# A hybrid attention and GLA step: softmax in merged operations, six split sums, turned keys beside the block scores, two attention steps per product, clock warm-up

## The chip, the cores and the metric

The kernel runs on one core of a Trainium2 chip. The metric is the device time of one execution in microseconds; before the change it is 2342.8 us, the median of 3 runs (2340.0 to 2345.78). A core has five engines that run beside each other, each with its own queue, and wait for one another through semaphores. TensorE (PE) multiplies matrices into PSUM, an accumulator memory of 8 banks; VectorE (DVE), ScalarE (ACT) and GpSimd (POOL) work element by element; SyncE (SP) starts DMA transfers between the chip's main memory and the on-chip memory SBUF.

## The reference, cut to what matters

One step of a two-layer encoder over 2048 prompt frames and 8 x 16 sample frames, width 1024. Each layer has window attention (A) and gated linear attention (GLA, B) side by side:

```python
u = rms_norm(h, norm_g) @ w_in
qa, ka, va, ga, qb, kb, vb, gb, ab = split(u)
qa = partial_rope(rms_norm(qa, q_norm_g), pos)      # 8 heads of 64
ka = partial_rope(rms_norm(ka, k_norm_g), pos)      # 2 heads of 64
# A: softmax over 192 keys, with a sink per head
m = maximum(max(s), sink); pr = exp(s - m)
oa = (pr / (sum(pr) + exp(sink - m))) @ va
# B: per block, b = cumsum(log_sigmoid(ab @ w_gate_up + b_gate) / 16)
att = where(causal, (qb * exp(b)) @ (kb * exp(-b)).T, 0)
ob = att @ vb + (qb * exp(b)) @ S
S = exp(b_last) * S + (kb * exp(b_last - b)).T @ vb
mix = concat([oa * silu(ga), rms_norm(ob, gla_norm_g) * silu(gb)])
h = h + mix @ w_out
h = h + sigmoid(rms_norm(h, pe_norm_g) @ w_pg) * (p @ w_pe)
```

Outputs are y, the last 128 rows of keys and values, and the states S.

## The kernel before, in words

**Tiling.** The 2176 frames are 17 tiles of 128 (the last holds the sample frames). `GROUPS` packs them into five groups of 3, 4, 4, 3 and 3 tiles; the two layers run over the five groups one after the other, 10 groups in all. Each group runs `phase_in` (the projection, attention, GLA, the first half of the output projection) and `phase_out` (the rest of it, the gate, the embedding).

**Products.** Every large product is made of three (`mm3`, L382 to L384), since each float32 operand is split into a rounded high half and a low half: high x high, high x low, low x high. `unit_a` gives 128 output columns for all frames of a group (24 products of 384 or 512 columns), `unit_b` 512 output columns for one tile. Weights come in pieces of 256 KB (`raw`); ScalarE rounds the high half (L212), VectorE subtracts the low half (L95). The weight ring holds five slots, and o-blocks (`o0` to `o3`, 256 columns of `w_out` each) take two.

**Banks.** Of the 8 PSUM banks two are the ring "mm" (`pm`), two the ring "t" (`pt`: transposes and other small products), and four change their use: while attention runs they are two pairs, "s" (scores) and "o" (outputs); elsewhere four single banks "w" (`pw1`).

**What is woven in between.** Attention and GLA are generators; after each large product `pump(n)` advances them by n steps, two lanes in turn, with n set by the table `Z` (`pga` after the attention gate's products). The program's text and these numbers give priorities; a scheduler with a timeline model then fixes each engine's order, so instructions can stand earlier or later than the text has them. On TensorE a queue runs strictly in that order: an instruction that waits holds up all behind it.

**Steps that the change touches.** `softmax` (L547 to L572): maximum, sink, negation (L559), four exponentials on ScalarE, sum, reciprocal, four scalings (L571). `gla_scores` (L823): the chain of block scores into "s", the masked copy `at` (L857), then two transposes of the keys (L860) into a bank of "t", copied to `ke` by ScalarE (L862). `gla_prompt`: output of a block into "o" (from `at` and the state S), the product with `ke` into "t", and S (L924); `gla_norm_gate` makes `on` (L875), `gla_out` transposes it (L886) and makes the second half of the mix (L888, L889). `fin` (L496): transposes of the keys and of the gate's low-rank input `ab`; kT is copied by ScalarE (L500), abT by VectorE (L501); `gate_chain` multiplies abT by `wgu` (L1073). At the end of `phase_in` (L1060 to L1066) the first halves (k 0 to 3, the attention half of the mix) of the first four output sums are made, the last tile's `gla_out` ("tail") before the fourth; `phase_out` adds the second halves and makes the other four sums whole.

## Time and profile before

| what | value |
|---|---|
| median of 3 runs | 2342.8 us |
| the profiled execution | 2341.45 us, its span 2339.7 us |
| TensorE busy | 2261.6 us, 97% |
| VectorE busy | 1622.7 us, 69% |
| ScalarE busy | 1271.1 us, 54% |
| GpSimd busy | 679.8 us, 29% |
| mean granted TensorE clock | 0.995 |
| DMA | 278.94 MB, mean 119 GB/s |

The span goes from the first to the last instruction. In the rows a tile stands as output<-inputs by the names of the program, and L is the line in the kernel before. Behind the bar or in brackets stands the time for which the engine was idle just before the instruction, and what ended that idle time. Matmuls are pipelined, so the durations of neighbours overlap, and the time from start to start is what one costs. A wait for several semaphores is put down to the one that came last.

### The profile page before, as it was taken

The page shows a single profiled execution, that of the slowest core. Times are in us where ns is not written, and L with a number is a line of the kernel's source. Part 1 is how long each engine was busy: PE and PEld are TensorE (multiplying, and loading weights), DVE is VectorE, ACT ScalarE, POOL GpSimd, SP SyncE. Part 2 cuts the span into 40 slices and gives each one's busy share as a digit, 9 for nine tenths or more (in the row PEclk, how much of TensorE's full clock was granted, in tenths as well). Part 3 has the DMA queues.
Part 4 walks back from the last instruction along what each step waited for, and adds up shares of the span by engine and source line. Part 5 has one row for each costly group of instructions (what it writes and reads, how often), then busy time and mean ns, then how long its engine had stood idle before and what let it go on. Part 6 is the DMA issues. An engine that isn't in the chain of part 4 may idle for free.

```text
span 2339.7 us, 41130 instructions
## 1 busy us (share of the span) xinstructions
PE 2261.6 (97%) x14796; PEld 1946.8 (83%) x14796; DVE 1622.7 (69%) x3579; ACT 1271.1 (54%) x2927; POOL 679.8 (29%) x771
## 2 busy tenths in 40 slices
PE   7999999999999999998999999999999999999998
PEld 6889877887778879887988898778877888798878
DVE  7757766768566866775776678667676678577755
ACT  6546544645545655553665556445554556566533
POOL 3124322342224222412331242224312142233222
PEclk9999999999999999999999999999999999999999
DMA  4334313433153425533542543234322443264343
GB/s 153 113 120 148 112 53 111 153 101 109 37 170 120 127 87 165 159 99 104 188 134 84 161 139 96 64 121 142 109 73 73 153 137 108 83 188 142 105 129 100
DMA packets 160236, 278.94 MB, mean 119 GB/s; under 512 B 17648, under 2 KB 43632, under 8 KB 160032
## 3 DMA queue, kind: packets, MB, share of 16 engines
q1 hardware_dynamic: 159344, 275.43, 38.1%
q8 instruction: 116, 1.90, 0.3%
q10 hardware_dynamic: 688, 0.88, 0.1%
q14 instruction: 88, 0.72, 0.1%
HBM read 255.41 MB, written 20.71 MB: 118 GB/s over the span
## 4 chain that ended last, share of the span: by engine, by line
PE 77%; DVE 6%; issue 6%; DMA 4%; ACT 4%; POOL 3%; DVEq 0%; ACTq 0%; POOLq 0%; SPq 0%
PE mm L382 15%; PE mm L384 14%; PE mm L383 14%; PE pw L382 7%; PE pw L383 7%; PE pw L384 7%; PE o L126 3%; DVE w L95 2%; DMA raw<-in_w_pe_dram 2%; PE s L120 2%; PE s L126 2%; POOL xacc L95 1%; DMA raw<-in_w_out_dram 1%; ACT w L212 1%; PE o L120 1%
## 5 line engine op out<-in xcount | busy, mean ns | idle before, releaser
L95 DVE TENSOR_TENSOR w<-raw,w 128x512 fp32r<-128x512 f32 (+1 forms) x800 | 575.3, 744 | 141.1 <-ACT w L212 136.3
L212 ACT ACTIVATE w<-raw 128x512 fp32r<-128x512 f32 (+1 forms) x800 | 471.4, 626 | 240.8 <-PE pw L384 62.5
L95 POOL TENSOR_TENSOR ot<-gth,hst 128x384 f32<-128x384 f32 (+1 forms) x79 | 102.3, 1300 | 290.6 <-DVE gth L1158 266.5
L382 PE MATMUL mm<-B,w 128*128 128x384 f32 (+1 forms) x432 | 156.3, 362 | 1.8 <-DVE gth L1154 1.1
L382 PE MATMUL mm<-A,w 128*128 128x384 f32 (+1 forms) x432 | 155.6, 360 | 1.9 <-DVE gth L1154 1.3
L384 PE MATMUL mm<-B,w 128*128 128x384 f32 (+1 forms) x432 | 156.1, 361 | 0.0
L383 PE MATMUL mm<-B,w 128*128 128x384 f32 (+1 forms) x432 | 155.9, 361 | 0.0
L384 PE MATMUL mm<-A,w 128*128 128x384 f32 (+1 forms) x432 | 155.6, 360 | 0.0
L383 PE MATMUL mm<-A,w 128*128 128x384 f32 (+1 forms) x432 | 155.0, 359 | 0.0
L382 PE MATMUL pw<-mix,w 128*128 128x384 f32 (+1 forms) x384 | 138.4, 366 | 12.0 <-DVE on L875 12.0
L95 POOL TENSOR_TENSOR acc<-sq,acc 128x384 f32<-128x384 f32 (+1 forms) x60 | 74.3, 1239 | 259.7 <-ACT sq L313 259.5
L382 PE MATMUL mm<-w,B 128*128 128x512 f32 (+1 forms) x368 | 141.7, 385 | 0.0
L383 PE MATMUL mm<-w,B 128*128 128x512 f32 (+1 forms) x368 | 141.3, 384 | 0.0
L384 PE MATMUL mm<-w,B 128*128 128x512 f32 (+1 forms) x368 | 140.8, 383 | 0.0
L382 PE MATMUL mm<-w,A 128*128 128x512 f32 (+1 forms) x360 | 139.5, 387 | 0.0
L383 PE MATMUL mm<-w,A 128*128 128x512 f32 (+1 forms) x360 | 138.8, 385 | 0.0
L384 PE MATMUL mm<-w,A 128*128 128x512 f32 (+1 forms) x360 | 138.3, 384 | 0.0
L384 PE MATMUL pw<-mix,w 128*128 128x384 f32 (+1 forms) x384 | 137.4, 358 | 0.0
L383 PE MATMUL pw<-mix,w 128*128 128x384 f32 (+1 forms) x384 | 137.3, 357 | 0.0
L95 POOL TENSOR_TENSOR mix<-ga_t,mix 128x512 fp32r<-128x512 f32 x34 | 53.0, 1560 | 265.6 <-ACT mix L583 265.6
L563 ACT ACTIVATE P<-s,mx 128x192 f32<-128x192 f32 (+3 forms) x272 | 108.7, 412 | 8.6 <-DVE mx L559 8.4
L1155 ACT ACTIVATE gth<-gth 128x384 f32<-128x384 f32 (+2 forms) x81 | 45.0, 560 | 125.7 <-DVE gth L1154 125.5
(320 smaller groups left out, 6378.7 us busy)
## 6 DMA issues: line engine op xcount, KB each, us to landing
raw<-in_w_in_dram SPq DMA_DIRECT2D x400, 256.0 KB, 2.9
raw<-in_w_out_dram SPq DMA_DIRECT2D x160, 256.0 KB, 2.9
raw<-in_w_pg_dram SPq DMA_DIRECT2D x160, 256.0 KB, 3.0
raw<-in_w_in_dram SPq DMA_DIRECT2D x40, 272.0 KB, 3.0
raw<-in_w_pe_dram SPq DMA_DIRECT2D x40, 256.0 KB, 3.3
hl<-in_h_dram SPq DMA_DIRECT2D x24, 192.0 KB, 3.2
hbuf<-ot SPq DMA_DIRECT2D x24, 192.0 KB, 1.9
hx<-hbuf SPq DMA_DIRECT2D x24, 192.0 KB, 3.8
```

The lines of the kernel that those rows point to most:

```text
L95: (eng or G).tensor_tensor(out=out, in0=in0, in1=in1, op=op1)
L120: prev[0] = PE.matmul(**kw).ins
L126: prev[0] = PE.matmul(**kw).ins
L212: A.activation(out=hi, in_=r, func=ACTF.Copy)
L382: PE.matmul(out=out, lhsT=sh, rhs=mh, start=first and i == 0, stop=False)
L383: PE.matmul(out=out, lhsT=sh, rhs=ml, start=False, stop=False)
L384: lastmm[0] = PE.matmul(out=out, lhsT=sl, rhs=mh, start=False, stop=last and i == n).ins
L563: A.activation(out=P[:, e, p0:p0 + wd], in_=ps[:, e // 2, e % 2, :wd], func=ACTF.Exp, scale=0.125, bias=mx[:, e:e + 1], accum_out=den[:, 0 ...
L1155: ta = A.activation(out=th[:, c], in_=th[:, c], func=ACTF.Tanh, scale=0.5)
```

## The change

**Softmax.** A negated copy of the sinks is made once (`nsink`, on GpSimd). The running maximum is then kept negated, which drops the negation (L559), and the four scalings of P become one operation with the reciprocals broadcast along the keys (two operations in the first tile, whose pieces have different widths).

**abT** is copied out of PSUM by ScalarE, behind kT, and no longer by VectorE.

**Turned keys.** The two transposes of `gla_scores` go into the free upper half of the pair "s" that the scores are written to, chained behind the scores; the masked copy waits for them too, and no bank of "t" is taken.

**Split sums.** At the end of `phase_in` six sums get their first half and not four: two in "mm", four in "w". For it, the first half of block o2 is split earlier (`w_get_part`), the rest in `phase_out` (`w_rest`).

**Steps per product.** `pga` goes from 1 to 2.

**Start.** The constants for the mean are made by VectorE; ScalarE copies one column early; 18 products of 256 columns with these constants are put ahead of all others on TensorE.

```diff
-Z = dict(eg=0, gk=2, yp=1, ym=6, pga=1, ...
+Z = dict(eg=0, gk=2, yp=1, ym=6, pga=2, ...
+    nsink = const.tile([128, DEPTH, V_TOT - V_SP], F32, name="nsink")
+    def wait_for(op, x):
+        tc.add_manual_dep(op, x.name, ..., reason="other products of the same banks")
+    def w_get_part(l, gi, nm):
+        bi = st["blk"]
+        while st["split"] < first_piece[bi] + 2:
+            assert w_split()
+        st["blk"] += 1
+        return Block(bi)
+    def w_rest(w):
+        while st["split"] <= last_piece[w.bi]:
+            assert w_split()
...
-                V.tensor_copy(abT[:, ti * TT:ti * TT + TT], p[0:96, 1, :])
+                A.activation(out=abT[:, ti * TT:ti * TT + TT], in_=p[0:96, 1, :], func=ACTF.Copy)
...
-            V.scalar_tensor_tensor(out=mv, in0=mv, scalar=0.125, in1=sink4, op0=ALU.mult, op1=ALU.max)
-            V.tensor_tensor(out=den[:, 1]..., in0=sink4, in1=mv, op=ALU.subtract)
-            V.tensor_scalar(out=mx, in0=mx, scalar1=-1.0, scalar2=None, op0=ALU.mult)
+            V.scalar_tensor_tensor(out=mv, in0=mv, scalar=-0.125, in1=nsink4, op0=ALU.mult, op1=ALU.min)
+            V.tensor_tensor(out=den[:, 1]..., in0=mv, in1=nsink4, op=ALU.subtract)
...
-            for e in range(4):
-                V.tensor_scalar(out=P[:, e, p0:p0 + wd], in0=P[:, e, p0:p0 + wd], scalar1=den[:, 0, e:e + 1], scalar2=0.5,
-                                op0=ALU.mult, op1=ALU.mult)
+                if wd_of is None:
+                    if c == 0:
+                        V.scalar_tensor_tensor(out=P, in0=P, scalar=0.5, in1=den[:, 0].unsqueeze(2).to_broadcast(P.shape),
+                                               op0=ALU.mult, op1=ALU.mult)
...
-            pa = pair("s")[:, :, :256].rearrange("p e (h t) -> p e h t", h=2)
+            ps2 = pair("s")
+            pa = ps2[:, :, :256].rearrange("p e (h t) -> p e h t", h=2)
+            pk = ps2[:, 1, 256:512]
...
+            for hp in range(2):
+                with tc.issue_after(pv[0]), tc.high_priority():
+                    pv[0] = PE.transpose(out=pk[:, hp * 128:hp * 128 + 128], in_=E[:, 2 if sample else 4, hp, :], identity=ident).ins
...
-            V.copy_predicated(av, m..., pa)
-            pk = pt([128, 256])
-            for hp in range(2):
-                PE.transpose(out=pk[:, hp * 128:hp * 128 + 128], in_=E[:, 2 if sample else 4, hp, :], identity=ident)
+            cp = V.copy_predicated(av, m..., pa)
+            wait_for(cp.ins, pv[0])
...
-            pss.append(unit_a(mixes, ws[mt // 2], mt % 2, 0, n, pm(n) if mt % 3 == 0 else pw1(n), ks=(0, 4), end=mt % 2 == 1))
+            pss.append(unit_a(mixes, ws[mt // 2], mt % 2, 0, n, pm(n) if mt < 2 else pw1(n), ks=(0, 4), end=mt % 2 == 1))
+        ws.append(w_get_part(l, gi, "o2"))
+        for mt in (4, 5):
+            pss.append(unit_a(mixes, ws[2], mt % 2, 0, n, pw1(n), ks=(0, 4), end=mt % 2 == 1))
...
-            if mt >= 4 and m == 0:
-                ws.append(w_get(l, gi, f"o{mt // 2}"))
+            if mt == 4:
+                w_rest(ws[2])
+            if mt == 6:
+                ws.append(w_get(l, gi, "o3"))
...
-            if mt < 4:
+            if mt < 6:
...
-        G.memset(ones_f, 1.0 / 1024)
-        V.tensor_copy(ones_r, ones_f)
+        G.tensor_scalar(out=nsink, in0=vec[:, :, V_SP:], scalar1=-1.0, scalar2=None, op0=ALU.mult)
+        V.memset(ones_f, 1.0 / 1024)
+        V.tensor_copy(ones_2, ones_f)
+        V.tensor_copy(ones_r, ones_f[:, :128])
+        A.activation(out=ones_f[:, 0:1], in_=ones_f[:, 0:1], func=ACTF.Copy)
+        warm = pm()
+        for i in range(18):
+            PE.matmul(out=warm[:, :256], lhsT=ones_r, rhs=ones_2, start=True, stop=True)
```

Since the scheduler fixes the order, the diff does not show where the instructions now stand. Three places on TensorE follow, each before and in the changed kernel; in the changed kernel all lines have other numbers.

The first group, near the end of `phase_in`: block scores (`s<-E`), turned keys (`<-cst,E`), attention output (`o<-ptf`, `o<-pth`) and the first block's output (`o<-vb,at`). Before:

```order
L384 MATMUL mm<-w,A_127 128x512
L860 MATMUL t<-cst,E 128x128 x2
L120 MATMUL o<-ptf,vT 64x256
L126 MATMUL o<-ptf,vT 64x256 x3
L126 MATMUL o<-pth,vT 64x256 x4
L120 MATMUL o<-vb,at_83 128x128
```

Now the transposes follow their scores, and products stand between the attention output and the block's:

```order
L131 MATMUL s<-E 32x64 x4
L875 MATMUL s<-cst,E 128x128 x2
L637 MATMUL t<-cst,P 128x128
...
L131 MATMUL o<-pth,vT 64x256 x4
L401 MATMUL mm<-w,A_151 128x512
...
L402 MATMUL mm<-w,A_151 128x512
L125 MATMUL o<-vb,at_84 128x128
```

The transposes have left the ring "t", and 23 large products now separate the two uses of the pair "o".

The end of the same group: the last tile's block (`o<-vb,at`), its update (`t<-vb,ke`), first half sums (`pw<-mix`) and the transposes of `on`. Before:

```order
L886 MATMUL t<-cst,on 128x128 x4
L120 MATMUL o<-vb,at_83 128x128
L126 MATMUL o<-vb,at_83 128x128 x3
L126 MATMUL o<-S,E 128x128 x4
L126 MATMUL t<-vb,ke 64x128 x4
L382 MATMUL pw<-mix_223,w 128x384
...
L384 MATMUL pw<-mix_223,w 128x384
L886 MATMUL t<-cst,on 128x128 x4
```

The left-out rows are two half sums, 24 products, then the tail's transposes. Now:

```order
L131 MATMUL t<-vb,ke 64x128 x4
L912 MATMUL t<-cst,on 128x128 x4
L400 MATMUL pw<-mix_247,w 128x384
...
L402 MATMUL pw<-mix_247,w 128x384
L912 MATMUL t<-cst,on 128x128 x4
L400 MATMUL pw<-mix_247,w 128x384
```

The transposes of the tile before have moved behind the last block, and the tail's stand after one half sum (12 products) instead of two; the other three half sums follow them.

The gate product of the fifth group (the first layer's, with the sample tile): transposes of the last tile's keys and gate input, then the product with abT. Before:

```order
L498 MATMUL t<-cst,yk 128x128
L499 MATMUL t<-cst,ab_77 96x128
L382 MATMUL mm<-w,A_9584 128x512
...
L384 MATMUL mm<-w,A_9585 128x512
L1073 MATMUL pw<-abT,wgu 128x384 x2
L382 MATMUL mm<-A_9584,w 128x384
```

Now:

```order
L516 MATMUL t<-cst,yk 128x128
L517 MATMUL t<-cst,ab_78 96x128
L1102 MATMUL pw<-abT,wgu 128x384
L1102 MATMUL mm<-abT,wgu 128x384
L400 MATMUL pw<-w,A_9484 128x512
```

The 15 products that stood ahead of the gate product now stand behind it.

More of the change, by code (lines that the diff above doesn't have):

```diff
@@ L114, in pair @@
         return banks["pool"].tile([128, 2, 512], F32, tag=tag, name=tag, bufs=1)
+    def wait_for(op, x):
+        tc.add_manual_dep(op, x.name, mybir.DependencyInfo(mybir.DependencyClass.Sync, mybir.DependencyReason.DATA),
+                          reason="other products of the same banks")
     def chain(prev, after=(), behind=None, **kw):
@@ L545, in phase_in, with softmax @@
         lock = set()
-        def softmax(ps, P, sink4, wd_of):
+        def softmax(ps, P, nsink4, wd_of):
             mx = ip.tile([128, 4], F32, tag="mx", name="mx", bufs=2)
@@ L556, in softmax @@
                     V.tensor_reduce(out=mv[:, :, c], in_=ps[:, :, c, :wd_of[c]], axis=AX.X, op=ALU.max)
-            V.scalar_tensor_tensor(out=mv, in0=mv, scalar=0.125, in1=sink4, op0=ALU.mult, op1=ALU.max)
-            V.tensor_tensor(out=den[:, 1].rearrange("p (i c) -> p i c", c=2), in0=sink4, in1=mv, op=ALU.subtract)
-            V.tensor_scalar(out=mx, in0=mx, scalar1=-1.0, scalar2=None, op0=ALU.mult)
+            V.scalar_tensor_tensor(out=mv, in0=mv, scalar=-0.125, in1=nsink4, op0=ALU.mult, op1=ALU.min)
+            V.tensor_tensor(out=den[:, 1].rearrange("p (i c) -> p i c", c=2), in0=mv, in1=nsink4, op=ALU.subtract)
             for e in range(4):
@@ L567, in softmax @@
             V.reciprocal(out=den[:, 0], in_=den[:, 0])
-            for e in range(4):
-                wd = P.shape[2] if wd_of is None else wd_of[e % 2]
-                p0 = 0 if wd_of is None else 128 - 64 * (e % 2)
-                V.tensor_scalar(out=P[:, e, p0:p0 + wd], in0=P[:, e, p0:p0 + wd], scalar1=den[:, 0, e:e + 1], scalar2=0.5,
-                                op0=ALU.mult, op1=ALU.mult)
+            dv = den[:, 0].rearrange("p (i c) -> p i c", c=2)
+            Pv = P.rearrange("p (i c) k -> p i c k", c=2)
+            for c in range(2):
+                if wd_of is None:
+                    if c == 0:
+                        V.scalar_tensor_tensor(out=P, in0=P, scalar=0.5, in1=den[:, 0].unsqueeze(2).to_broadcast(P.shape),
+                                               op0=ALU.mult, op1=ALU.mult)
+                else:
+                    p = Pv[:, :, c, 128 - 64 * c:128 - 64 * c + wd_of[c]]
+                    V.scalar_tensor_tensor(out=p, in0=p, scalar=0.5, in1=dv[:, :, c:c + 1].to_broadcast(p.shape),
+                                           op0=ALU.mult, op1=ALU.mult)
         def gate_mix(ot, ti, C):
@@ L604, in attn_prompt @@
                               rhs=kk[gs, k0:k0 + wd], start=True, stop=True)
-                sink = vec[:, l, V_SP + hp:V_SP + 4:2].unsqueeze(2).to_broadcast([128, 2, 2])
+                sink = nsink[:, l, hp:4:2].unsqueeze(2).to_broadcast([128, 2, 2])
                 softmax(lst, P, sink, [64, 128] if first else None)
@@ L673, in attn_sample @@
                                       start=True, stop=True)
-                sink = vec[:, l, V_SS + g:V_SS + g + 1].unsqueeze(2).to_broadcast([128, 2, 2])
+                sink = nsink[:, l, 4 + g:5 + g].unsqueeze(2).to_broadcast([128, 2, 2])
                 softmax(lst, P, sink, None)
@@ L1195, in hybrid_step @@
         SP.dma_start(out=vec, in_=a["vec"])
[L1196 to L1198 removed]
+        G.tensor_scalar(out=nsink, in0=vec[:, :, V_SP:], scalar1=-1.0, scalar2=None, op0=ALU.mult)
+        ones_f = pp.tile([128, 256], F32, name="ones_f")
+        V.memset(ones_f, 1.0 / 1024)
+        ones_2 = pp.tile([128, 256], F32R, name="ones_2")
+        V.tensor_copy(ones_2, ones_f)
[4 more added lines that the diff above has]
+            PE.matmul(out=warm[:, :256], lhsT=ones_r, rhs=ones_2, start=True, stop=True)
         px = prep_x(pp, 0, 0, "A", nx, True)
```

6 lines of the change are left out of this document (3 added, 3 removed).

## The prediction

> **What bounds the kernel now.** I read the page first, then the list of waits for TensorE alone, then the timeline at the places that this list names. The page:
>
> ```profile
> span 2339.7 us, 41130 instructions
> ...
> PE 2261.6 (97%) x14796; PEld 1946.8 (83%) x14796; DVE 1622.7 (69%) x3579; ACT 1271.1 (54%) x2927; POOL 679.8 (29%) x771
> ```
>
> TensorE is busy in 97% of the span, and the change takes no product away. So it can only win back TensorE's idle time, 2339.7 - 2261.6 = 78.1 us, and time in which products run at a low clock. VectorE and ScalarE have room: work taken off them counts only where TensorE waits for it. The list of TensorE's waits, first after 45 us, then for the first 45 us (what waited, what it waited for, us in total, times, longest):
>
> ```profile
> PE pw L382 <- DVE on L875: 12.0, 10, 1.9
> PE t L886 <- DVE on L875: 7.8, 4, 2.7
> PE t L860 <- DVE S L924: 6.6, 4, 1.7
> PE s L120 <- issue: 4.6, 2, 2.9
> PE t L860 <- DVE mix L889: 4.5, 4, 1.3
> PE o L120 <- DVE ga_t L582: 3.9, 4, 1.0
> ...
> PE mm L1073 <- DVE abT L501: 2.9, 2, 1.4
> ...
> PE pw L1073 <- DVE abT L501: 1.4, 1, 1.4
> ```
> ```profile
> PE mm L480 <- ACT w L212: 7.8, 1, 7.8
> PE t L498 <- DVE abT L501: 5.4, 2, 3.8
> PE t L528 <- DVE yq L461: 1.3, 1, 1.3
> PE mm L481 <- DVE w L95: 1.2, 1, 1.2
> ```
>
> The second list sums to 15.7 us, the first with its left-out rows to 57; the 5.4 us that are missing to 78.1 I take to be the end, after the last product. After the start no single wait is over 2.9 us, and no row names the softmax (tile P): its latency is already hidden.
>
> **Turned keys in the scores' banks.** Before, the two transposes of L860 take a bank of the ring "t", and TensorE stands until S (L924) or mix (L889) has been read out of it: 6.6 + 4.5 = 11.1 us in 8 places. Now they follow the block scores in the same two banks "s" that these hold already, so there is no ring bank to wait for: **-11.1 us**. Ends: 0 if the wait only moves to the next taker of "s", -11.1 otherwise. The added wait (the mask copy L857 now also waits for the two transposes) delays a vector operation whose reader, the product of L910, stands 12 or more products behind; on VectorE the next operations of the block (its exponents' products, the next `on`) queue behind it. Uncovered it would be about 0.3 us each, 34 times. The copy ke on ScalarE now holds "s"; the next scores come several products later.
>
> **More attention steps per product.** Only the order moves. At the four places of the row "o <- ga_t" (3.9 us), the block output used to follow the attention output of the same banks at once; in the change's order at least 16 products lie between: **-3.9 us** (ends 0 and -3.9). That P is wanted sooner I price at nothing for the lack of a row on P; the uncovered price is in the slower rival.
>
> **Six split sums.** The diff reads as if two more half sums would fill the wait of L875. The order says otherwise. The scheduler before had already put the first half of the fifth sum and two thirds of the sixth ahead of the second halves. And in both kernels one product stands between the last tile's blocks and the first instruction that needs the tile's `on`. The first group's end:
>
> ```profile
> 149.53 0.66 PE L126 MATMUL t<-vb,ke 128*64 128x128 f32 x8
> ...
> 150.11 0.45 PE L382 MATMUL pw<-mix,w 128*128 128x384 f32 x1
> ...
> 152.92 1.13 DVE L875 SCALAR_TENSOR_TENSOR on<-o,gss,sgb 128x128 f32<-128x128 f32 x4 [2.08 <-POOL gss L872]
> ...
> 154.10 0.45 PE L382 MATMUL pw<-mix,w 128*128 128x384 f32 x1 [1.63 <-DVE on L875]
> ...
> 156.32 0.60 PE L886 MATMUL t<-cst,on 128*128 128x128 f32 x4
> ```
>
> `on` ends at 154.05, 3.9 us after the last block product. Before, the second half sum in the banks of "o" waited for it; now the last tile's transposes do, after as many products. In three of the four three-tile groups the previous tile's transposes have moved into the gap (0.5 us less to wait, by the 0.60 of the last row with its overlap); in the fourth 12 more products lie there too (all 1.6 less); in the four four-tile groups those transposes have moved out of it (0.45 more each); in the two groups with the sample tile nothing moves. Sum: -1.5 - 1.6 + 1.8, about **-1.3 us** instead of -12. Ends: -12 and +4. The two weight pieces of o2 that VectorE now splits earlier stand in the 2.08 us that it is idle there.
>
> **abT on ScalarE.** One group, before:
>
> ```profile
> 772.88 0.27 PE L499 MATMUL t<-cst,ab 128*96 128x128 f32 x1
> ...
> 773.53 0.27 ACT L500 ACTIVATE kT<-t 128x128 f32<-128x128 f32 x1
> ...
> 774.27 0.28 DVE L501 CAST abT<-t 96x128 fp32r<-96x128 f32 x1
> ```
>
> VectorE began its copy only 0.47 us after ScalarE's had ended. With both on ScalarE I expect the gate product about 0.5 us sooner, so a wait near 0.95 us for 1.44. But the order has moved: the gate product now directly follows its last transposes in three groups, follows 3 or 4 products later in three, and has room in the others. 3 x 0.95 + 3 x 0.2 = 3.4 us against the 4.3 of the two rows: **-0.9 us** (ends -4.3 and +3).
>
> **The start.** Before:
>
> ```profile
> 3.92 1.28 ACT L350 ACT_TABLE_LOAD   x1 [3.92 <-DMA vec<-in_vec_dram]
> ...
> 7.76 0.60 PE L480 MATMUL mm<-w,A 128*128 128x272 f32 x1 [7.76 <-ACT w L212]
> ...
> 15.24 0.43 PE L482 MATMUL pw<-w,A 128*128 128x272 f32 x1
> 15.47 0.43 PE L481 MATMUL pw<-w,A 128*128 128x272 f32 x1
> ...
> 18.83 0.28 PE L480 MATMUL mm<-w,A 128*128 128x272 f32 x1
> 18.95 0.29 PE L481 MATMUL mm<-w,A 128*128 128x272 f32 x1
> ...
> 22.52 0.39 PE L382 MATMUL mm<-w,A 128*128 128x512 f32 x1
> ```
> ```profile
> 15.57 0.71 DVE L95 TENSOR_TENSOR w<-raw,w 128x544 fp32r<-128x544 f32 x1
> ...
> 20.01 0.55 DVE L95 TENSOR_TENSOR ah<-xacc,ah 128x384 fp32r<-128x384 f32 x1
> ```
>
> The table load waits for `vec`; now a one-column copy brings it in before that, so all of ScalarE's first work and the first product move up by 1.28 us, to about 6.5 (unless the transfer of h that ScalarE issues behind the load comes too late: then nothing). Products start every 0.23 us at 15 us and every 0.12 at 19: the clock rises 9.5 us after the first product. The 18 warm-up products take 18 x 0.21 = 3.8 us (256 columns at the early pitch for 272) and lie in TensorE's idle 7.8 us. With the clock up, weights bind: the fourth piece's low half comes at 16.28 - 1.28 = 15.0 and 18 products follow it. I take 19.0 for the end of the kv products, and for q the end of `ah`, 20.56 - 1.28 = 19.3: 2.9 us sooner than 22.52. The Trainium skill ("TensorE: Matmul & The Clock Gate", part 1, the HAM clock gate) says that the clock rises after one busy window of about 3.4 us whose phase is free. By that rule 3.8 us of products fill a whole window only by luck, and where they do not, the gain there would be nearer 1.3 us. The 9.5 us above, with a pause in it, agree that a few busy microseconds need not be enough.
>
> Then comes the hole in which the three tiles' keys are transposed:
>
> ```profile
> 33.44 0.27 PE L498 MATMUL t<-cst,yk 128*128 128x128 f32 x1
> ...
> 34.21 0.31 ACT L500 ACTIVATE kT<-t 128x128 f32<-128x128 f32 x1
> 34.53 1.28 ACT L282 ACT_TABLE_LOAD   x1
> ...
> 35.83 0.58 ACT L282 ACTIVATE nyx<-t,epst 128x384 f32<-128x384 f32 x1
> ...
> 42.46 0.67 PE L1073 MATMUL pw<-abT,wgu 96*128 96x384 f32 x1
> ```
>
> From the first transpose to the gate product it takes 9.0 us. In the change's order ScalarE does kT, abT, a table load and a pass, twice, and kT, abT: 0.8 + 0.6 + 2 x (1.9 + 0.6) = 6.4 us, 2.6 less; the four q transposes that stood in this chain now stand behind 24 products. 2.9 + 2.6 = 5.5, of which I give 1 back to the clock, which falls in the hole:
>
> ```profile
> 38.00:42.00 4.00, 1.00 (x4) 0.57 (x5) 3.72 (x12) 0.69 (x3) 1.07 (x2) 0.50 0.00 0
> ```
>
> (a stretch, its length, busy time of PE, PEld, DVE, ACT, POOL; granted clock 0.50). **-4.5 us**; ends -1.3 and -8.
>
> **Merged softmax operations.** Four scalings of 192 columns become one of 768 with a broadcast second operand:
>
> ```profile
> L571 DVE TENSOR_SCALAR P<-P,den 128x192 f32<-128x192 f32 x240 | 67.2, 344 | 1.7
> ...
> L1111 DVE SCALAR_TENSOR_TENSOR phl<-pr,phl 128x768 fp32r<-128x768 f32 x6 | 5.8, 959 | 15.8 <-ACT phl L1110 15.8
> ```
>
> 67.2 / 60 = 1.12 us for four against 0.96 for the nearest row of the new kind: VectorE wins some 0.2 us per softmax and the negation, TensorE **nothing**.
>
> **New waits.** Each order of this program has its own places in which TensorE is a microsecond short: 57 us over 10 groups, some 1.2 us a place. Two or three new ones I expect: **+3 us** (ends 0 and +12). Sum: -11.1 - 3.9 - 1.3 - 0.9 - 4.5 + 3 = **-18.7 us**. The profiled execution took 2341.45 us (its span and 1.75 around it), 1.35 under the median of 2342.8; against the median I forecast **2324.1 us**.
>
> **Rivals.** *The waits of L875 go after all* (the tail's transposes find `on` ready because VectorE and ScalarE are earlier everywhere): the other 10.7 us of the first row go too, and a few of the 7.8 of the second: 2311. For it: the row is the largest; against it: the chain to `on` starts at TensorE's own last block product and is not shortened. Chance 0.17. *The waits move and do not go*: what L860 waited for, VectorE's reads behind weight splits, is met at the next instruction; only the start's gain stays: 2338. For it: TensorE has no slack to lose a wait into; against it: the eight places have products ready behind them. Chance 0.14. *Slower, by the single pair of banks "s"*: 68 softmaxes and 34 blocks take it in turn, it is now held until ke is copied, and two steps per product bring the takers closer together. Each take that finds it occupied costs TensorE the rest of that holding; 102 takes at 0.3 us (a copy like that of kT, 0.27 above) are +31 us, so 2324 + 31 = 2355, and it decides from 0.19 us a take (18.7 / 102). Against it: no row of waits for "s" is there before. Chance 0.06.
>
> **How the numbers follow.** Forecast 0.63. Each rival but the first lies above 2335.8 us, that is 0.3% under the median, about what a measurement of this kernel can tell from no change. Faster: 0.63 + 0.17 and a little of the second rival's spread, 0.81; same 0.14; slower 0.05. The range leaves out the last rival and the outer ends: 2308 to 2339.
>
> **What would show it.** In the changed kernel's list of TensorE's waits: no row on the transposes of E; no row "o <- ga_t", or one much shorter; rows on `on` that sum to some 18 us still, now nearly all on transposes; rows on abT near 3 us after the start. At the start the first kv product near 6.5 us, and the gate product of the first group near 37. The forecast is wrong if rows on "s" or P appear, or if the rows on `on` vanish.

## The result and the profile after

The changed kernel takes **2319.4 us** (median; 2318.2 to 2322.4) beside 2342.9 for the kernel before in the same comparison: ratio 0.9902, 95% interval 0.9885 to 0.9919. The forecast was 2324.1, with a range of 2308 to 2339. The time and the sign were right; most of the reasons were not: the two largest terms of the sum are wrong, a small one was in truth the largest, and the errors cancel.

The page of the changed kernel and its list of TensorE's waits (what waited, what it waited for, us in total, times, longest). L901 is `on`, L912 its transposes, L888 `ke`, L519 `abT`, L125 the first product of a chain:

```profile
span 2320.7 us, 40960 instructions
...
PE 2268.3 (98%) x14814; PEld 1953.6 (84%) x14814; DVE 1605.0 (69%) x3279; ACT 1272.2 (55%) x2962; POOL 671.0 (29%) x771
```
```profile
PE t L912 <- DVE on L901: 9.2, 13, 1.9
PE o L125 <- ACT ke L888: 7.0, 6, 2.4
PE mm L498 <- ACT w L217: 4.5, 2, 3.6
PE pw L1102 <- ACT abT L519: 3.4, 3, 1.7
PE s L125 <- ACT qs L548: 3.4, 1, 3.4
...
PE o L125 <- ACT w L217: 1.3, 1, 1.3
```

All waits of TensorE sum to 47.5 us where the list before had 72.7: 25.3 less. Against this TensorE is 6.7 us longer busy: 4.2 us are the 18 warm-up products, most of the rest is more time at the half clock. With 0.3 us less at the end that is, to within 0.1 us, the 19.0 by which the span is shorter.

What the list shows against the one of before:

- The transposes of E (11.1 us) are gone from it, and `ga_t` (3.9) too.
- A new row stands there: the block product waits for `ke`, 7.0 us in 6 places, with a seventh under the name of a weight split (1.3).
- The two rows on `on` fell from 19.8 to 9.2 us. The prediction had left 18 of them.
- The start has a new wait of 3.6 us in this execution; in a second execution of the same kernel (the last section) it is 1.3 us.

**Where the turned keys' wait went.** One of the six places, in order of time (start, us, engine, line, operation; in brackets the idle time before it and what ended it):

```profile
872.35 0.44 PE L875 MATMUL s<-cst,E 128*128 128x128 f32 x2
...
875.34 0.75 DVE L915 SCALAR_TENSOR_TENSOR mix<-t,vec,mix 128x512 fp32r<-128x512 f32 x1 [0.83 <-ACT mix L914]
...
876.31 0.87 DVE L901 SCALAR_TENSOR_TENSOR on<-o,gss,sgb 128x128 f32<-128x128 f32 x3 [0.22 <-POOL gss L898]
877.10 0.71 DVE L885 COPY_PREDICATED at<-mk,s 128x512 f32<-128x512 uint8 x1
...
877.84 0.38 ACT L888 ACTIVATE ke<-s 128x256 f32<-128x256 f32 x1 [2.54 <-DVE at L885]
...
878.28 0.49 PE L125 MATMUL o<-vb,at 128*128 128x128 f32 x2 [2.36 <-ACT ke L888]
```

The keys are turned at 872.8, without any wait. Their copy `ke` starts 5 us later: it reads the banks that the masked copy `at` reads, and in this program stands behind it. `at` in turn stands on VectorE behind `S`, `mix` and three of the four operations of `on`, which wait for GpSimd. ScalarE idles 2.54 us, TensorE 2.36.

**Where the waits on `on` went.** The end of a group of four tiles, first in the changed kernel, then in a kernel with four sums instead of six (an experiment below). In both, GpSimd's last operation on `gss` ends at the same distance, and `on` begins at once:

```profile
657.34 0.66 PE L131 MATMUL t<-vb,ke 128*64 128x128 f32 x8
...
660.68 1.13 DVE L901 SCALAR_TENSOR_TENSOR on<-o,gss,sgb 128x128 f32<-128x128 f32 x4 [2.03 <-POOL gss L898]
...
661.18 1.01 PE L912 MATMUL t<-cst,on 128*128 128x128 f32 x4 [0.23 <-DVE on L901]
...
661.95 0.48 PE L400 MATMUL pw<-mix,w 128*128 128x512 f32 x1
```
```profile
654.21 0.66 PE L131 MATMUL t<-vb,ke 128*64 128x128 f32 x8
...
657.55 1.13 DVE L901 SCALAR_TENSOR_TENSOR on<-o,gss,sgb 128x128 f32<-128x128 f32 x4 [2.02 <-POOL gss L898]
...
658.73 0.50 PE L400 MATMUL pw<-mix,w 128*128 128x512 f32 x1 [0.92 <-DVE on L901]
```

With four sums the next product takes the banks "o" and needs all four operations of `on`: it starts 1.18 us after they begin. With six sums the tail's transposes come next, and the first of them needs only the first of the four: it starts after 0.50 us, and the four transposes are done while `on` goes on. In both, 12 products of the mix stand ahead of this place. From the last block products to the product of the mix that is shown here it takes 4.61 us in the one and 4.52 in the other, but in the one the transposes (0.60 us) are then behind it, in the other they are still to come.

**The start.** ScalarE in the changed kernel:

```profile
1.22 1.28 ACT L1233 ACT_TABLE_LOAD   x1 [1.22 <-PEq L1367]
2.07 0.44 ACTq L348 DMA_DIRECT2D hfull<-in_h_dram  x1
...
9.19 1.63 ACT L368 ACTIVATE A<-hfull,vec 128x384 fp32r<-128x384 f32 x3 [2.03 <-DMA hfull<-in_h_dram]
```

The table load has come between ScalarE's two transfers of `h`. The second is issued at 2.07 us, ScalarE waits for it until 9.19, and TensorE waits 3.60 us for the weights behind it, at 13.76 us. In the second execution of this kernel the order is the same, but ScalarE waits until 8.89 and TensorE 1.27 us, at 13.47. The first product of the weights is at 7.21 us, the first group's gate product at 40.8 (42.5 before), where 6.5 and 37 had been forecast.

### The profile page after: what moved, and what is told of

The parts are those of the page before. It is cut to its first block, busy times and chain, and to the rows that moved or that the text cites. A ratio compares the mean times of both kernels' runs of the same rounds, so it can differ in the third digit from the quotient of the medians.

```text
span 2320.7 us, 40960 instructions
## 1 busy us (share of the span) xinstructions
PE 2268.3 (98%) x14814; PEld 1953.6 (84%) x14814; DVE 1605.0 (69%) x3279; ACT 1272.2 (55%) x2962; POOL 671.0 (29%) x771
## 4 chain that ended last, share of the span: by engine, by line
PE 83%; ACT 4%; DVE 4%; DMA 4%; issue 3%; POOL 2%; ACTq 0%; DVEq 0%; POOLq 0%; SPq 0%
PE mm L400 15%; PE mm L402 15%; PE mm L401 14%; PE pw L400 9%; PE pw L401 9%; PE pw L402 9%; PE o L131 3%; DVE w L96 2%; PE s L131 2%; PE s L125 2%; DMA raw<-in_w_pe_dram 1%; DMA raw<-in_w_out_dram 1%; PE o L125 1%; ACT gsq L895 1%; ACT w L217 1%
## 5 line engine op out<-in xcount | busy, mean ns | idle before, releaser
L400 PE MATMUL mm<-B,w 128*128 128x384 f32 (+1 forms) x440 | 160.8, 365 | 1.1 <-DVE yq L470 0.8
L402 PE MATMUL mm<-B,w 128*128 128x384 f32 (+1 forms) x440 | 159.8, 363 | 0.0
L401 PE MATMUL mm<-B,w 128*128 128x384 f32 (+1 forms) x440 | 159.0, 361 | 0.0
L400 PE MATMUL pw<-mix,w 128*128 128x384 f32 (+1 forms) x424 | 153.0, 361 | 0.0
L401 PE MATMUL pw<-mix,w 128*128 128x384 f32 (+1 forms) x424 | 151.2, 357 | 0.0
L402 PE MATMUL pw<-mix,w 128*128 128x384 f32 (+1 forms) x424 | 151.0, 356 | 0.0
L400 PE MATMUL mm<-A,w 128*128 128x384 f32 (+1 forms) x408 | 148.5, 364 | 2.0 <-DVE yq L470 1.8
L402 PE MATMUL mm<-A,w 128*128 128x384 f32 (+1 forms) x408 | 148.0, 363 | 0.0
L401 PE MATMUL mm<-A,w 128*128 128x384 f32 (+1 forms) x408 | 147.8, 362 | 0.0
L400 PE MATMUL mm<-w,B 128*128 128x512 f32 (+1 forms) x360 | 137.9, 384 | 0.0
L402 PE MATMUL mm<-w,B 128*128 128x512 f32 (+1 forms) x360 | 137.7, 383 | 0.0
L401 PE MATMUL mm<-w,B 128*128 128x512 f32 (+1 forms) x360 | 137.4, 382 | 0.0
L96 POOL TENSOR_TENSOR mix<-ga_t,mix 128x512 fp32r<-128x512 f32 x34 | 43.9, 1290 | 283.1 <-ACT mix L606 283.1
```

Of the source, the lines that this page charges most:

```text
L96: (eng or G).tensor_tensor(out=out, in0=in0, in1=in1, op=op1)
L400: PE.matmul(out=out, lhsT=sh, rhs=mh, start=first and i == 0, stop=False)
L401: PE.matmul(out=out, lhsT=sh, rhs=ml, start=False, stop=False)
L402: lastmm[0] = PE.matmul(out=out, lhsT=sl, rhs=mh, start=False, stop=last and i == n).ins
```

## The experiments

Each kernel was timed in five rounds beside the kernel before, whose median was 2340.6 to 2344.2 us; what is compared is the ratio to it. The changed kernel itself gave 0.9902 and, taken again, 0.9895; 0.9898 stands for it below. A ratio's interval reaches some 0.0014 to either side, so that 4 to 5 us between two of these kernels are needed to tell them apart.

| kernel | median us | ratio, interval | against the changed kernel |
|---|---|---|---|
| changed, again | 2318.2 | 0.9895, 0.9881 to 0.9908 | |
| early copy behind the transfers | 2317.4 | 0.9884, 0.9871 to 0.9898 | -3.3 us |
| ke ahead of at | 2318.8 | 0.9888, 0.9873 to 0.9904 | -2.3 |
| keys in the ring "t" again | 2323.1 | 0.9910, 0.9897 to 0.9924 | +2.8 |
| four sums | 2333.2 | 0.9948, 0.9935 to 0.9960 | +11.7 |
| six sums alone, on the kernel before | 2333.6 | 0.9965, 0.9952 to 0.9977 | (-8.2 against before) |
| one step per product of ga | 2325.4 | 0.9929, 0.9917 to 0.9942 | +7.3 |
| early copy behind, at ahead of on | 2315.6 | 0.9889, 0.9874 to 0.9904 | -2.1 |
| early copy behind, shorter chain to on | 2339.9 | 0.9989, 0.9979 to 0.9999 | +21.3 |
| four scalings | 2319.8 | 0.9904, 0.9887 to 0.9921 | +1.4 |
| start as before | 2315.4 | 0.9883, 0.9866 to 0.9899 | -3.5 |
| start as before, abT on VectorE | 2315.2 | 0.9883, 0.9867 to 0.9900 | -3.5 |

(The last column is the difference of the ratios times 2342.9.)

### The late transfer

```diff
-        A.activation(out=ones_f[:, 0:1], in_=ones_f[:, 0:1], func=ACTF.Copy)
         warm = pm()
...
         next(px)
+        A.activation(out=ones_f[:, 0:1], in_=ones_f[:, 0:1], func=ACTF.Copy)
```

> The changed kernel with one line moved: ScalarE's early one-column copy is written behind the issue of the four transfers of h instead of ahead of them, so that its table load no longer stands between ScalarE's two transfers. In the changed kernel the second of them is issued at 2.07 us (before: directly behind the first, 0.72 to 1.70) and ScalarE then waits until 9.19 for it; TensorE waits 3.6 us at 13.76 and the clock falls to half until 20.8. Theory (the late transfer costs it): ScalarE's wait of 2.03 us shrinks below 0.5, TensorE has no wait over 1.5 us between 7 and 20 us, the first-row keys' products end near 20.5 instead of 23.9, and the span is 3 to 4 us shorter: about 2316. Rival (the transfers share one bandwidth, so that the order of issue does not matter, and the fall of the clock comes from the weights): the waits stay within 0.5 us and the time within 1 us, 2319.

ScalarE at the start of this kernel:

```profile
0.72 0.98 ACTq L348 DMA_DIRECT2D hfull<-in_h_dram  x2
...
7.35 1.61 ACT L368 ACTIVATE A<-hfull,vec 128x384 fp32r<-128x384 f32 x3
```

ScalarE's wait for the second transfer is gone, TensorE's longest wait between 7 and 20 us is 1.5 us, and the mean's product, behind the keys' products, stands at 20.6 us instead of 23.9. So the late transfer costs time there, but in other runs less than these 3.3 us: in the second execution of the changed kernel the mean's product stands at 22.3, and in the two later kernels that have this repair too (`at` ahead of `on`, the shorter chain) at 22.0. The gate product of the first group comes at 39.9 us (40.8), and the time is 3.3 us better, under what can be told.

### The start undone

```diff
-        V.memset(ones_f, 1.0 / 1024)
...
-        warm = pm()
-        for i in range(18):
-            PE.matmul(out=warm[:, :256], lhsT=ones_r, rhs=ones_2, start=True, stop=True)
+        G.memset(ones_f, 1.0 / 1024)
+        V.tensor_copy(ones_r, ones_f)
```

> The changed kernel with the start of the kernel before: no warm-up products, no early one-column copy, the ones written by GpSimd. By the prediction's sum 4.5 us slower, 2323. Theory from the two traces (the warm-up and the earlier table load were given back by ScalarE's late second transfer; at the first group's gate product 1.7 us are left of the gain, of which 0.9 may be abT's): 1 to 2 us slower, 2320, the first product at 7.8, the keys' products' end at 22 to 23 and the clock at half until 17.

Neither was right: without the new start the kernel is not slower, but 3.5 us faster in the median, which is less than can be told. The first product is at 8.09 us and the mean's product at 22.7, 2.1 us later than in the run with the repaired start (0.7 later than in the two other kernels that have it), and yet the first group's gate product comes at 39.6, as early as there (39.9). What lies between is the hole in which the keys are transposed. Its chain stands on ScalarE, with two table loads in it (ScalarE's timeline of this kernel):

```profile
35.18 1.28 ACT L300 ACT_TABLE_LOAD   x1
...
37.40 1.28 ACT L301 ACT_TABLE_LOAD   x1
```

Products that come sooner wait there longer: TensorE's row of transposes behind abT is 4.1 us with the repaired start and 2.6 here. The gain of 2.9 us that the first group keeps over the kernel before has nothing to do with the new start.

### abT, beside it

```diff
-                A.activation(out=abT[:, ti * TT:ti * TT + TT], in_=p[0:96, 1, :], func=ACTF.Copy)
+                V.tensor_copy(abT[:, ti * TT:ti * TT + TT], p[0:96, 1, :])
```

> The kernel of the run with the start as before, and in it abT written by VectorE again as well: what is left of the change is the turned keys, the six sums, the merged softmax operations and the two steps per product. Against the run with the start as before (2315.4 us). Theory (in that run the first group's gate product came at 39.6 us against 42.5 in the kernel before, with the same start: that gain is abT's, together with the order of the transposes around it): the gate product of the first group goes back to about 42.5, the other groups' rows on abT rise from 2.6 to about 4.3 us, and the time is 3 to 4.5 us longer, 2319. By the prediction's sum 2.6 us of it belong to the start's hole and 0.9 to the rest: 2319 as well. Rival (the 2.9 us in the first group come from the order alone): within 1.5 us of 2315.4.

The gate product of the first group went back to 42.7 us, as the theory said, and the rows on abT after the start rose from 2.6 to 5.2 us: abT on ScalarE is worth some 3 us in the hole and 2.6 behind it. The time is the same all the same (0.9883 both). The list of TensorE's waits of this kernel shows which rows fell in return, and not why: the row on `ke` is 3.8 us here and 7.8 in the run above, that on `on` 7.6 and 8.7. All waits together are 48.3 us here and 46.1 there.

```profile
PE t L912 <- DVE on L901: 7.6, 10, 1.9
PE t L516 <- DVE abT L519: 5.4, 2, 3.9
PE o L125 <- ACT ke L888: 3.8, 6, 0.8
```

### The turned keys

```diff
+            pk = pt([128, 256])
+            for hp in range(2):
+                PE.transpose(out=pk[:, hp * 128:hp * 128 + 128], in_=E[:, 2 if sample else 4, hp, :], identity=ident)
```

(in their old place, and the change's two transposes, `pk` and `wait_for` taken out)

> The changed kernel with the turned keys alone put back: the two transposes of E take a bank of the ring t again, the masked copy waits for nothing more than before. Theory from the two traces (the wait of 11.1 us went, but 8.3 us came back as waits for ke and a like one): this kernel is about 3 us slower than the changed one, 2322, with rows of TensorE on the transposes of E near 11 us and none on ke. By the prediction's sum it would be 11 us slower, 2330.

From the list of TensorE's waits of this kernel (L883 the transposes of E, L909 those of `on`):

```profile
PE t L883 <- DVE S L947: 11.8, 7, 2.0
PE t L909 <- DVE on L898: 7.9, 11, 1.8
```

The row on the transposes of E is back with 11.8 us, and the one on `ke` is gone, all of its 7 to 8 us. All waits together sum to 46.2 us against 47.5. The time is 2.8 us longer, within what can't be told from nothing, while the 11 us of the prediction's sum could be told. The 11 us were there; they were not to be had.

### The order of the two readers

```diff
+            ke = ip.tile([128, 256], F32, tag="ke", name="ke", bufs=3 if is_sample(tiles[-1]) else 2)
+            done["ke"] = A.activation(out=ke, in_=pk, func=ACTF.Copy).ins
             cp = V.copy_predicated(av, m.unsqueeze(1).unsqueeze(1).to_broadcast([128, 2, 2, 128]), pa)
             wait_for(cp.ins, pv[0])
-            ke = ip.tile([128, 256], F32, tag="ke", name="ke", bufs=3 if is_sample(tiles[-1]) else 2)
-            done["ke"] = A.activation(out=ke, in_=pk, func=ACTF.Copy).ins
```

> The changed kernel with the two readers of the banks s in the other order: ScalarE's copy ke first, VectorE's masked copy at second. In the changed kernel ke waits for the masked copy (33.4 us of ScalarE's idle time in 17 of 34 places), which itself stands in VectorE's queue behind on, S and mix; the block product then waits 7.0 us in 6 places for ke (a place at 143.9 with 1.3 us is of the same kind). Theory (the wait of the turned keys was moved to ke by this order): ke comes straight behind the transposes, the rows o<-ke fall below 2 us, what the product then waits for is at, 2 to 3 us in all; about 4 us faster, 2315. Rival (the masked copy is what is late, and the product needs it as well as ke): the 7 us stay, under the name at, and the time stays within 1.5 us of 2319.

From the same list of this kernel (L887 is `at` here):

```profile
PE o L125 <- DVE at L887: 6.3, 6, 2.7
```

The rival: `ke` is early now, and the wait stands unchanged under the name `at`. The copy `ke` was only the last link.

### at ahead of on

```diff
+                with tc.issue_after(done["cp"]):
                     V.scalar_tensor_tensor(out=on[:, h, :], in0=po[:, h % 2, h // 2, :], scalar=ss[:, h:h + 1], in1=...
```

(with the early copy behind the transfers, as above)

> The changed kernel with two edits: the early one-column copy behind the issue of the transfers of h, as in the first experiment, and the last tile's operations on bound to stand behind the masked copy at of the following tile on VectorE. TensorE's order is the same as in the changed kernel; in the groups of three tiles at now stands ahead of on, which waits for GpSimd anyway. Theory (the waits for ke come from at standing behind on on VectorE): the waits of 2.36 us at 878.3 and of 1.71 at 2021.6 fall below 1 us each, the small ones in the four groups of four tiles (0.6 to 0.8) stay, since there at still stands behind on; with the start's gain about 2314, 2 to 3 us under the first experiment's 2317. Rival (what delays ke is ScalarE or the products themselves): the waits stay and the time is that of the first experiment.

From the same list of this kernel (L902 is `on`):

```profile
PE o L125 <- DVE on L902: 4.3, 3, 1.7
...
PE o L125 <- ACT ke L888: 3.1, 4, 0.8
```

The waits for `ke` at 878.3 and 2021.6 went, as the theory said, and stand as waits of 1.69 and 1.59 us at the same products, now for `on`: the block product takes the banks "o", and `on` reads the tile before out of them. So three conditions come within a microsecond of each other there, `ke`, `at` and the banks, and all three hang on the same stretch of VectorE's queue, which waits for GpSimd. Taking one away uncovers the next. In time this run is not told from the one with the repaired start alone (0.9889 and 0.9884), from which 2 to 3 us had been expected.

### The six sums

```diff
-            if mt < 6:
+            if mt < 4:
                 ps = unit_a(mixes, ws[mt // 2], m, 0, n, pss[mt], ks=(4, 8), end=m == 1)
```

(with `w_get_part`, the fifth and sixth first halves and `w_rest` taken out)

> The changed kernel with four split sums instead of six: the fifth and sixth sum of the mix are again not cut in halves. Theory from the two traces (the waits for on fell from 19.8 to 9.2 us, since the tail's transposes need the first of the four on operations only, while a half sum in the banks o needed all four): the waits for on go back to 17 to 20 us, the time is 8 to 10 us longer, about 2328. By the prediction's sum the six sums are worth 1.3 us: 2321.

The two rows on `on` in the list of TensorE's waits of this kernel:

```profile
PE pw L400 <- DVE on L901: 10.5, 10, 1.6
...
PE t L912 <- DVE on L901: 6.3, 4, 1.9
```

The waits for `on` are back at 10.5 + 6.3 and another 1.3 under "o", 18.1 us, and the time is 11.7 us longer. The row on `ke` is longer too, 9.8 us for 7.0. The other way round, the six sums alone on the kernel before:

> The kernel before with the six split sums alone (the fifth and sixth sum cut in halves, both halves' banks as in the change). By the prediction's sum: 1.3 us faster than before. Theory from the run with four sums (11 us slower than the changed kernel): the rows of waits for on fall from 19.8 to about 10 us and the time by 8 to 11 us, to about 2333; the rows on the transposes of E (11.1 us), ga_t (3.9) and abT stay as they are in the kernel before.

From the list of this kernel (L899 the transposes of `on`, L873 those of E, L1172 the first operation on `gth`), and a row on `gth` from the list of the kernel before, where that operation is L1154:

```profile
PE t L899 <- DVE on L888: 11.4, 9, 2.5
...
PE t L873 <- DVE S L937: 6.7, 4, 1.8
...
PE pw L395 <- DVE gth L1172: 1.7, 3, 0.7
```
```profile
PE pw L382 <- DVE gth L1154: 3.3, 4, 1.3
```

8.2 us faster than before, with the other rows of the kernel before still there (E behind S 6.7 and behind mix 4.8, ga_t 3.9 us). The rows on `on` fell by 8.4 us: from 1.6 or 1.9 to 0.95 in each group of three tiles, from 0.57 to nothing in each group of four, from 10.8 to 7.6 in the two with the sample tile. About half of this returns as transposes that stand longer (21.6 us for 17.4), since they go at the pace of `on`.

The six sums change a second place as well. In `phase_out` TensorE waits for banks until VectorE has read the gate's and the embedding's products out of them (`gth`, two operations). All rows on `gth` sum to 8.9 us in the kernel before and to 8.0 in the one with four sums; here they are 3.7, in the changed kernel 4.7, and in each of the twelve executions with six sums between 2.2 and 4.7. How much of the 8 to 12 us belongs to this place no run separates.

### Two steps per product

```diff
-Z = dict(eg=0, gk=2, yp=1, ym=6, pga=2,
+Z = dict(eg=0, gk=2, yp=1, ym=6, pga=1,
```

> The changed kernel with one attention step instead of two per product of the blocks ga. By the prediction's sum: 3.9 us slower, 2323, with a row of TensorE on ga_t near 3.9 us back. Rival (the wait for ga_t was one of several near places, and the scheduler finds another order either way): the row comes back and the time stays within 1.5 us of 2319.

From the list of TensorE's waits of this kernel:

```profile
PE t L912 <- DVE on L901: 16.8, 12, 2.1
PE o L125 <- DVE on L901: 3.6, 4, 1.0
...
PE o L125 <- DVE ga_t L605: 2.6, 4, 1.0
```

7.3 us slower, more than the row. `ga_t` returns with 2.6 us, but the rows on `on` rise from 9 to 20.4, and that on `ke` vanishes: I read it so that with the attention steps later the tiles' blocks are later, too, and their last waits fall elsewhere; no run shows this by itself.

### The merged scaling

```diff
-                        V.scalar_tensor_tensor(out=P, in0=P, scalar=0.5, in1=den[:, 0].unsqueeze(2).to_broadcast(P.shape),
-                                               op0=ALU.mult, op1=ALU.mult)
+            for e in range(4):
+                V.tensor_scalar(out=P[:, e, p0:p0 + wd], in0=P[:, e, p0:p0 + wd], scalar1=den[:, 0, e:e + 1], scalar2=0.5,
+                                op0=ALU.mult, op1=ALU.mult)
```

> The changed kernel with the merged scaling of P undone: four operations of 192 columns instead of one of 768 (the merged negation stays). By the prediction's sum it is worth nothing to TensorE: VectorE busy about 8 us more (1.12 against 0.96 us a time, and the shares of the sample tiles), the time within 1.5 us of 2318. Rival (VectorE's queue is what at and on wait in, so 0.15 us in each of 68 softmaxes counts at the places behind): 2 to 4 us slower, 2321.

1.4 us slower, not told from nothing; VectorE is 10.5 us longer busy (1615.5). The changed kernel's row of the merged operation:

```profile
L590 DVE SCALAR_TENSOR_TENSOR P<-P,den 128x768 f32<-128x768 f32 x64 | 61.7, 964 | 1.8
```

### A shorter chain to on

```diff
-            for h in range(4):
-                A.activation(out=gq, in_=po[:, h % 2, h // 2, :], func=ACTF.Square, accum_out=ss[:, h:h + 1])
-            G.tensor_scalar(out=ss, ...
+            A.activation(out=on.rearrange("p (h e) t -> p e h t", e=2), in_=po, func=ACTF.Square)
+            V.tensor_reduce(out=ss, in_=on, axis=AX.X, op=ALU.add)
+            V.tensor_scalar(out=ss, ...
```

(with the early copy behind the transfers)

> The changed kernel with two edits: the early one-column copy behind the transfers of h, as in the first experiment, and a shorter chain from a tile's block products to its on. Now: four squares with their sums on ScalarE (4 x 0.47 us), two operations on GpSimd (0.35 and 1.01). In this kernel: one square of 512 columns on ScalarE (0.6 by the row of ptf), the sum on VectorE (about 0.65 by the rows of mx and qrs), the scaling on VectorE (0.2 to 0.3), the power on GpSimd as it is (1.01): about 2.5 us for 3.15, 0.5 to 0.6 less. Theory (the waits for on, 9 us in 12 or 13 places, and a part of the block product's 8 us are bound by this chain): the rows on on fall by 0.5 us a place to 3 or 4 us, the time by 5 to 7 us against the first experiment, to about 2311. Rival (VectorE's new operations stand in front of weight splits and of at, and ScalarE's square waits for the buffer of on): the gain is eaten, 2316 or more.

The same list of this kernel, and the chain of the first group's last tile in its timeline (L894 the square, L895 the sum, L897 the scaling, L899 the power):

```profile
PE t L913 <- DVE on L902: 20.6, 14, 4.6
PE o L125 <- DVE on L902: 9.4, 4, 3.3
```
```profile
146.34 0.60 ACT L894 ACTIVATE on<-o 128x512 f32<-128x512 f32 x1 [2.87 <-PE o L131]
...
147.40 0.61 DVE L951 SCALAR_TENSOR_TENSOR S<-S,dec,t 128x128 f32<-128x128 f32 x2 [2.55 <-PE t L131]
147.92 0.68 DVE L895 TENSOR_REDUCE gss<-on 128x4 f32<-128x512 f32 x1
...
149.01 0.75 DVE L916 SCALAR_TENSOR_TENSOR mix<-t,vec,mix 128x512 fp32r<-128x512 f32 x1 [0.41 <-ACT mix L915]
...
149.68 0.28 DVE L897 TENSOR_SCALAR gss<-gss,cols 128x4 f32<-128x4 f32 x1
...
150.10 1.01 POOL L899 TENSOR_TENSOR gss<-gss,mhalf 128x4 f32<-128x4 f32 x1 [7.62 <-DVE gss L897]
```

The operations are as short as reckoned, and the chain is longer: 4.77 us from the square to the end of the power, where the four squares and GpSimd's two operations took 3.1 (657.53 to 660.65 in the changed kernel). The sum waits behind `S`, the scaling behind `mix`, which itself waits for ScalarE. This is the rival, and dearer than it said: 21 us against the changed kernel, 25 against the one with the repaired start, from which it differs by the chain alone. TensorE's waits at the block products and at the transposes of `on` sum to 33.9 us in 22 places, where that kernel has 19.1 in 20, and the time at half clock, 34.1 us for 23.9, adds some 5 more by half of the difference. The run bears out one half of the theory, with the sign turned round: what is added to this chain, TensorE pays for.

## Why the prediction was right, and where it was not

- **Turned keys, -11.1 us: wrong.** Undone, they are worth 2.8 us, which can't be told from nothing. The step that failed is the choice of the end: the prediction had given 0 "if the wait only moves to the next taker of 's'", and took the other. The wait moved to the product that reads `at` and `ke`. Two sentences of that part were mistaken: that 12 or more products cover `at` (at the place shown above, the products behind the transposes end at 875.92 us, 1.9 us before `at` is done, since `at` queues behind `on` on VectorE), and that the copy `ke` is as free as the one of kT (it stands behind `at`, by the banks that both read). The rival "the waits move and do not go" described this part.
- **Six sums, -1.3: wrong, by the most.** Alone they gave 8.2 us, undone 11.7. The step said that the tail's transposes would wait for `on` "after as many products" and priced only what stood in the gap. It left out that the banks "o" are free after four operations of `on` and a transpose is ready after one. So the groups of four, which were to wait 0.45 us longer each, wait 0.2 us for 0.57 in the changed kernel, and the two groups with the sample tile, in which nothing was to move, went from 10.8 to 7.6 us with the six sums alone. The rows on `gth` were not in the sum at all. The forecast that some 18 us would stay on `on` went with it: 9.2. The rival "the waits of L875 go after all" had the size right and the reason wrong: `on` is no earlier, it is needed in pieces behind the same 12 products.
- **The start, -4.5: wrong, there is no gain** (+3.5, whose sign can't be told; the 8 us between the two can). The condition was named ("unless the transfer of h comes too late") and should have decided: the text of the change has the early copy, and with it the table load, ahead of that transfer's issue. But with the transfer repaired no gain can be told either, because what the products come sooner (2.1 us in one run and 0.7 in two, for the 2.9 forecast) is waited off in the hole. Its second half, 2.6 us less in the hole, went as said and further: with the start as before it takes 5.6 us from the first transpose to the gate product where it took 9.0, and with abT on VectorE again 9.0 as well.
- **More attention steps, -3.9: the row went as said**, and undone they are worth 7.3 us: a mis-sized term, since the step counted only the product that waited and not what the blocks behind it then meet.
- **abT, -0.9: the rows went from 4.3 to 2.6 us**, each 0.85 where 0.95 was forecast; in time it is worth nothing that can be told.
- **Softmax, 0: right.** The merged operation took 0.96 us, as reckoned, and its cover held.
- **New waits, +3:** yq (1.85 us at 532.0), qs (3.36 at 1203.5) and ah (2.16 at 218.7) are longer or new, and each was followed by a stretch at half clock, which began within 1.4 us of the wait's end. In the second execution the wait for qs is 1.8 us. The 8.3 us on `ke` were new, too. No run measures this term by itself.

The parts undone one by one make 11.7 + 7.3 + 2.8 + 1.4 - 3.5 = 19.7 of some 24 us (abT, undone beside the start, adds nothing). What the remaining 4 are can't be said; the runs leave about as much open in each term. The forecast of the time held because -11.1 for 2.8, -4.5 for +3.5 and -1.3 for 11.7 happen to balance. That is luck: with one of these errors alone it would have been 8 to 10 us off. The slower rival (the single pair "s") has nothing for it: no row of waits for "s" as a bank appeared.

Open stays how the gain of the six sums divides between `on` needed in pieces and the waits for `gth`: the rows on `on` account for 8.4 us, 4.2 of which return as slower transposes, those on `gth` for some 3 to 5, while other rows grew. No run delayed the transposes alone.

The start as before with all other parts (2315.4 us) beats the kernel before by 0.0117 of its time, and the changed one by less than can be told.

## What to carry to other kernels

A wait that is taken away is worth only its distance to the next condition of the same work: list all that the waiting product and the next three need, and when each is there, before writing the row off. When two products can stand next, choose the one that needs the first piece of a result, not the one that needs the whole bank. In a queue that runs in order, an operation that is itself short can make the chain longer; count what stands ahead of it, not its duration.

## What the runs showed of the hardware

**The clock and short waits.** The changed kernel was run a second time, unaltered:

> The changed kernel once more, unaltered, beside the next three. Both theories: about 2319 us and the same list of TensorE's waits, each row within 1 us. What it tells is how far two executions of one kernel differ in the windows of half clock (31.4 us in 8 windows in the first profile): if these are set by waits of 1.8 us and more alone, they stand at the same places again; if their phase is free, some places with a wait of 1.5 to 2.2 us have one now and others not, and the span moves by 1.7 us for each.

Two profiled executions of the changed kernel differ by 5.7 us in span (2320.7 and 2315.0). By the clock's records in the two traces the first has 30.7 us at half clock (where the expectation says 31.4), the second 21.0: half of the difference is 4.9 us. Not every row of waits came back within 1 us: that on the first weights is 4.5 us in the one and 2.6 in the other, that on qs 3.4 and 1.8. The places of the half clock are not the same either. Two of them, first in the one, then in the other (a stretch, its length, busy time of PE, PEld, DVE, ACT, POOL, the granted clock, the transfers' share and GB/s); the wait ahead of the stretch at 2020.9 was 1.71 us in the first execution and 2.27 in the second, ahead of the one at 1092.2 it was 1.87 and 1.84:

```profile
2020.90:2024.40 3.50, 2.80 (x29) 2.39 (x29) 2.12 (x6) 2.22 (x8) 0.00 (x0) 1.00 0.15 23
1092.20:1095.70 3.50, 3.50 (x23) 2.72 (x22) 1.36 (x3) 1.66 (x9) 0.00 (x0) 0.51 0.28 79
```
```profile
2020.90:2024.40 3.50, 3.50 (x21) 3.00 (x20) 1.19 (x4) 2.17 (x9) 1.35 (x2) 0.51 0.49 150
1092.20:1095.70 3.50, 3.50 (x28) 2.89 (x28) 1.18 (x3) 1.48 (x8) 1.02 (x3) 1.00 0.38 112
```

In the 14 profiled executions, after 45 us, a wait of TensorE of 1.2 to 1.7 us was followed by half clock within 3 us of its end in 7 of 78 cases (stretches that began during the wait are counted), one of 1.7 to 2.0 us in 32 of 59, one of 2.0 to 2.5 in 18 of 33, a longer one in all 11. Each stretch lasts 3.4 us or a multiple of it. By an estimate, a stretch costs up to half its length, where TensorE has work all through it, so that a wait of 1.8 us costs 1.8 or up to 3.5.

The Trainium skill ("TensorE: Matmul & The Clock Gate", part 1, the HAM clock gate) names an idle window of about 3.4 us, of free phase, after which the clock is halved. The free phase and the length of the stretches agree with the traces; that 1.7 to 2.0 us of waiting were enough in 32 of 59 cases does not follow from what it states.

**The warm-up.** The 18 products end near 6.3 us. In the first execution 15 products ran between 8 and 10 us, which is the full clock's pace; in the second 10, hardly more than the 9 of the kernel before (busy times of TensorE first, with the number of products; the first execution, then the second):

```profile
8.00:10.00 2.00, 1.99 (x15) 1.92 (x15) 0.17 (x1) 0.81 (x2) 0.00 (x0) 1.00 1.05 400
```
```profile
8.00:10.00 2.00, 2.00 (x10) 1.93 (x10) 0.84 (x2) 1.11 (x3) 0.00 (x0) 1.00 1.06 398
```

The 1.00 for the clock in the second row is no measurement: the trace has no record of the clock before its first change, which in this execution comes at 17.3 us, and the view then takes it as full. The products show the half clock there: they start 0.23 us apart up to 17.2 us and 0.12 behind it.

So some 4 us of products raise the clock in one execution and not in another. In the ten executions that have them the first rise stands at 5.3 to 6.8 us in five and at 11.0 to 17.3 in the others; in the four without them it stands at 11.0 to 17.4. And here even the raised clock bought nothing that shows: the mean's product stands at 20.6 to 23.9 us in the first five, at 22.0 to 24.6 in the other five and at 22.2 to 22.7 in the four. In the first execution above TensorE then waited 3.60 us for weights, and the clock fell to half from 13.7 to 20.5 us.
